# Twenty-nine instead of twelve filler transposes in the opening, one load for three constants, and a new order of the last scalings and stores

## The chip, the cores and the metric

The kernel runs on one core of a Trainium2 chip. The metric is the device time of one execution in microseconds (us), the median of the runs shown. Everything is computed in fp32; a matrix product is made of three products of a high and a low part (the type F32R in the code), so that one product of the reference is three matmuls on the chip.

## The reference, cut to what matters

The layer has 1024 latent tokens and 256 context tokens of width 1024. The parts that the change touches are the first and the last:

```python
c_silu = jax.nn.silu(c)[:, None, :]
cctx_silu = jax.nn.silu(c_ctx)[None, :]
sh1, sc1, g1, sh2, sc2, g2 = jnp.split(c_silu @ w_ada[l] + b_ada[l], 6, axis=-1)
hx = _modulate(_rmsnorm(x, norm1_g[l]), sh1, sc1)      # (y * g) * (1 + sc1) + sh1
(xq, xk, xv, ...) = jnp.split(hx @ w_in[l], IN_OFFSETS, axis=-1)
...                                                     # attention, retention, merge
x = x + g2 * _conv_ffn(hx2, w_up[l], conv_w[l], conv_b[l], w_down[l])
return _rmsnorm(x, final_norm_g)                        # y = x * rsqrt(mean(x*x) + EPS) * g
```

The inputs `c` and `c_ctx`, the bias `b_ada` and the gains `norm1_g`, `norm2_g` are the small constants of the change. The last RMSNorm, whose rows are scaled and stored at the very end, is its third part.

## The kernel before, in words

The work runs in stages: an opening (0 to about 60 us) that normalizes and transposes the tokens, computes the modulation and starts the first projection; then neighbourhood attention, retention, merge and the feed-forward network with its down projection (`steps`, and the last loop of the file), which ends with the final RMSNorm. TensorE (PE) is busy in nearly the whole span.

**The opening** is written out by hand as a list of small steps under `manual_schedule`, so that each engine gets its instructions in the order of the list. The steps that matter here:

- `load_x(tb)` brings a block of 128 tokens (512 KB) by the queue of SyncE (SP); `load_ag(g, q)` brings a piece of 512 KB of the modulation's weights, `load_f(half, t)` a piece of the first projection's weights, by the same queue. The framework gives every DMA of SP's and ACT's queues the next of eight semaphores in turn; a DMA that gets a semaphore for the second time is issued only when the DMA that had it before has landed. So the small loads of the constants take part in this rotation.
- `square_x` (ACT) sums the squares of a block, `rstd_x` (POOL) makes the factor, `scale_x` (DVE) scales the block, `transp(tb, kbs)` (line 213) transposes pieces of it on PE into PSUM.
- `silu_cc` (line 260) makes the SiLU of the two conditioning vectors; `ag_mm(g, q)` (line 291) multiplies them by a piece of modulation weights, 8 small matmuls side by side; `ag_ev` copies the rows out, `ag_tr` (line 301) turns them into columns, `ag_fin` (lines 307 and 308) adds the bias and multiplies by the gain.
- `split_hi`, `split_lo` split weights in two parts, `mod_h`, `mod_v`, `mod_l` make the modulated tokens in two parts, and `first_mm(half, kb)` (lines 130 to 132) is the first projection: 9 matmuls of 128x512 for one block of 128 channels.
- `turn_idle(to, n)` (line 203) puts n transposes of the identity matrix on PE. Nothing reads their result. They stand at two places before the change: 34 ahead of the first transpose of tokens, 12 ahead of `ag_mm(0, 0)`.

**The constants** come by ACT's queue, in three DMAs: `ccol` (64 bytes in each of 128 partitions, for `silu_cc`), `bcol` (192 bytes, the bias) and `gcol` (64 bytes, the gains). Behind them on ACT stands the first activation (line 257), which loads a table.

**The end.** The last 512 tokens are four row blocks, here b = 0 to 3, and of each the right half of the columns comes last. For b = 0 to 2 the loop makes the last matmuls of block b; `vec` (DVE) multiplies by the gate and subtracts (lines 2413, 2414); `square` (ACT, line 2323) sums the squares; `factor` (POOL, lines 2332, 2333) makes the reciprocal root; `scaled` scales the left half on ACT (line 2340) and the right half on DVE (line 2341) and stores both, 256 KB each. Block 3 goes in two halves of 256 columns (lines 2430, 2431, 2433). Before the change `scaled` of block 1 stands between the two halves of block 3, `scaled` of block 2 behind them, and `scaled` of block 3 alternates: scale left part, scale right part, store the left part by ACT's own queue, store the right part by SP's queue, twice.

Of the kernel before, what the change touches and what calls it, by code (L numbers as in the profile page):

```python
# [8 lines left out]
F32 = mybir.dt.float32  # L9
F32R = mybir.dt.float32r  # L10
AF = mybir.ActivationFunctionType
ALU = mybir.AluOpType
# [4 lines left out]
P = 128  # L17
D = 1024
KB = D // P
# [15 lines left out]
EPS = 1e-6  # L35
# [5 lines left out]
def tile_hybrid_layer(ctx, tc: tile.TileContext, io, dbg=None):  # L41
    nc = tc.nc
    vec, act, pool, pe, sync = nc.vector, nc.scalar, nc.gpsimd, nc.tensor, nc.sync

    def sb(name, side, bufs=1):
        return tc.alloc_tile_pool(name=name, bufs=bufs, side=side, reuse_waits="tile")
# [25 lines left out]
    cpool = sb("const", "left")  # L72
# [5 lines left out]
    def const(name, shape, queue=None):  # L78
        t = cpool.tile(shape, F32, name=name)
        (queue or sync).dma_start(t, io[name])  # L80
        return t
# [75 lines left out]
    s0 = sb("start", "right")  # L157
# [15 lines left out]
    def rstd_x(t0, n):  # L173
        r = rstd[:, t0 : t0 + n]
        pool.tensor_scalar(r, ssq[:, t0 : t0 + n], 1.0 / D, EPS, ALU.mult, ALU.add)
        pool.tensor_tensor(r, r, mhalf[:, t0 : t0 + n], ALU.pow)
# [16 lines left out]
    def p_tile(tag):  # L193
        return p0.tile([P, 512], F32, tag=tag, bufs=2 if tag == "tp" else 3, name=tag)
# [6 lines left out]
    def turn_idle(to, n):  # L201
        for _ in range(n):
            pe.transpose(to, ident, ident)

    def transp(tb, kbs, tags=None, idle=0):
        grid, half, i = tb < NTB, tb // 4 % 2 if tb < NTB else 0, tb % 4 if tb < NTB else tb - NTB
        for n, kb in enumerate(kbs):
            if i == 0 and (grid or kb % 2 == 0):
                tps[grid, half, kb] = p_tile(tags[n])
                if not grid:  # L210
                    tps[grid, half, kb + 1] = tps[grid, half, kb][:, C:]
            turn_idle(tps[grid, half, kb][:, i * P : (i + 1) * P], idle)
            pe.transpose(tps[grid, half, kb][:, i * P : (i + 1) * P], xs[tb][:, kb * P : (kb + 1) * P], ident)
# [30 lines left out]

    ccin = s0.tile([P, KB, 2], F32, name="ccin")
    ccol = s0.tile([P, KB, 32], F32, name="ccol")
    vec.memset(ccol, 0.0)
    cs2 = csp.tile([P, D], F32, name="cs")  # L250

    cst = {}
    act.dma_start(ccin, io["ccol"])
    for k, name, shape in (("b", "bcol", [P, 48]), ("g", "gcol", [P, 2, KB])):
        cst[k] = const(name, shape, act)

    act.activation(tick, mhalf[:, 0:1], AF.Silu)

# [16 lines left out]
    def load_ag(g, q):  # L275
        ag[g, q] = s_tile("x", 19)
        sync.dma_start(ag[g, q], io["w_ada1g"][sum(QS[:g]) + q])
# [6 lines left out]
    def ag_mm(g, q, idle=0):  # L284
        nk = len(GROUPS[g])
        if q == 0:
            arow[g] = p_tile("tp")
            turn_idle(arow[g][:, 0:P], idle)
        for n in range(4):
            k, r = (4 * q + n) // nk, slice(32 * n, 32 * n + 32)  # L290
            pe.matmul(arow[g][r, 0:256], ccol[:, k], ag[g, q][:, n * 256 : n * 256 + 256], start=q == 0, stop=q == QS[g] - 1, tile_position=(0, 32 * n))
# [33 lines left out]
    def split_hi(half, t):  # L325
        act.copy(first[t][half][:, 0], fraw[half, t])
# [328 lines left out]
    with tc.manual_schedule():  # L655
# [17 lines left out]
        transp(0, (5,), ("c1",))  # L673
        transp(0, (4,), ("c0",))
        transp(0, (1,), ("c0",))
        ag_mm(0, 0, idle=12)
        rstd_x(3, 1)
        load_ag(1, 0)
        square_x(1)
# [61 lines left out]
        ag_ev(2, "act")  # L741
        evac_t(True, 0, 4, "vec")
        load_ag(3, 0)
        transp(1, (2,), ("c1",))
        split_hi(0, 1)
        ag_tr(2)
        split_hi(0, 2)
        ag_mm(4, 0)
        load_ag(3, 1)
        split_lo(0, 1)  # L750
        ag_fin(2)
# [263 lines left out]
    bcol, gcol = cst["b"], cst["g"]  # L1015
# [346 lines left out]
    mix, last = None, (None, None)  # L1362
    share = shares()
    for h in range(RH):
        head = Head(h)
        for i in range(NCB + NTB):
# [3 lines left out]
            last = (head, i)  # L1370
# [247 lines left out]
    for n, (db, half) in enumerate(order):  # L1618
        if n in (5, 6):
            k = len(wpn) - KH  # L1620
# [68 lines left out]
    last = len(gu) - 1  # L1689
# [458 lines left out]
    with tc.manual_schedule():  # L2148
# [4 lines left out]
        ts, vr = slice(3 * P, 4 * P), [gtile(0, F32, "vr").rearrange("p (k t) -> p k t", t=P) for _ in range(2)]  # L2153
# [127 lines left out]
    fg = dp.tile([P, D], F32, name="fg")  # L2281
    sync.dma_start(fg, io["final_g"].to_broadcast([P, D]))
    gate2 = brow(3, dp.tile([P, D], F32, name="gate2"))
    ssf = dp.tile([P, NTB, 6], F32, name="ssf")
    QB = NTB // 2
# [21 lines left out]
    def gs(dh):  # L2307
        return slice(dh * 512, dh * 512 + 512)
# [11 lines left out]
    part = {}  # L2320

    def square(tb, dh, junk):
        act.activation(junk, part[tb, dh], AF.Square, accum_out=ssf[:, tb, dh : dh + 1])

    def early_part(tb, dh):
        s, z = ssf[:, tb], part[tb, dh]
        pool.tensor_scalar(s[:, 2:3], s[:, dh : dh + 1], 1.0 / D, EPS, ALU.mult, ALU.add)
        pool.tensor_tensor(z, z, fg[:, gs(dh)], ALU.mult)

    def factor(tb, c):  # L2330
        s = ssf[:, tb]
        pool.tensor_scalar(s[:, 3:4], s[:, c : c + 1], 1.0 / D, s[:, 2:3], ALU.mult, ALU.add)
        pool.tensor_tensor(s[:, 4:5], s[:, 3:4], mhalf[:, 0:1], ALU.pow)

    def scaled(tb, dh):
        s, ts = ssf[:, tb], slice(tb * P, (tb + 1) * P)
        z0, z1 = part[tb, 1 - dh], part[tb, dh]
        last = tb == QB - 1
        for c in (slice(0, 256), slice(256, 512)) if last else (slice(0, 512),):
            act.activation(z0[:, c], z0[:, c], AF.Copy, scale=s[:, 4:5])  # L2340
            vec.scalar_tensor_tensor(z1[:, c], z1[:, c], s[:, 4:5], fg[:, gs(dh)][:, c], ALU.mult, ALU.mult)
            (act if last else sync).dma_start(io["out"][ts, gs(1 - dh)][:, c], z0[:, c])
            sync.dma_start(io["out"][ts, gs(dh)][:, c], z1[:, c])

    def finish(tb, dh):
        factor(tb, dh)
# [14 lines left out]
    for b in range(QB):  # L2361
        x, z = rows_of(b, 0), dw_tile("x2", NTB)
# [14 lines left out]
    for b in range(QB):  # L2377
        x, z = rows_of(QB + b, 1), dw_tile("x2", NTB)
# [8 lines left out]
    for b in range(QB):  # L2387
        tb = QB + b
        x, z = rows_of(tb, 0), dw_tile("z", 6)
# [9 lines left out]
    with tc.manual_schedule():  # L2399
        tl = [operands(6, j) for j in range(NH - NL, NH)]  # L2400
        halves = (slice(0, 256), slice(256, 512))
        for b in range(QB):
            ts = slice(b * P, (b + 1) * P)
            z, junk = dw_tile("z", 6), dw_tile("xr", 4)
            part[b, 1] = z
            if b == QB - 1:
                break
            for i, (a, w) in enumerate(tl):
                open3(banks[0][b], a[:, 0, ts], a[:, 1, ts], w[:, 0], w[:, 1], False, i == NL - 1)
            if b == 0:  # L2410
                for tb in range(NTB - 3, NTB):
                    finish(tb, 0)
            vec.tensor_tensor(z, banks[0][b], gate2[:, gs(1)], ALU.mult)
            vec.tensor_tensor(z, p1[b], z, ALU.subtract)
            square(b, 1, junk)
            if b == 0:
                rest = p1[QB - 1]
                vec.tensor_tensor(u2[QB - 1], banks[0][QB - 1], gate2[:, gs(1)], ALU.mult)
                vec.tensor_tensor(rest, rest, u2[QB - 1], ALU.subtract)
            else:  # L2420
                factor(b - 1, 1)
                if b < QB - 2:
                    scaled(b - 1, 1)
        ends = [pd[1].tile([P, 512], F32, tag="y", bufs=4, name="y")[:, 0:256] for _ in halves]
        for bank, c in zip(ends, halves):
            for i, (a, w) in enumerate(tl):
                open3(bank, a[:, 0, ts], a[:, 1, ts], w[:, 0, c], w[:, 1, c], i == 0, i == NL - 1)
        factor(b - 1, 1)
        for n, (bank, c) in enumerate(zip(ends, halves)):
            vec.tensor_tensor(z[:, c], bank, gate2[:, 512 + c.start : 512 + c.stop], ALU.mult)  # L2430
            vec.tensor_tensor(z[:, c], rest[:, c], z[:, c], ALU.subtract)
            k = 5 if n else 1
            act.activation(junk[:, c], z[:, c], AF.Square, accum_out=ssf[:, b, k : k + 1])
            if not n:
                s = ssf[:, b]
                pool.tensor_scalar(s[:, 2:3], s[:, 1:2], 1.0 / D, s[:, 2:3], ALU.mult, ALU.add)
                scaled(b - 2, 1)
        scaled(b - 1, 1)
        factor(QB - 1, 5)
        scaled(QB - 1, 1)  # L2440
    pd[1].release()
    pd[0].release()
    dp.release()
# [9 lines left out]
def layout(inputs):  # L2453
    import numpy as np

    g = {k: np.asarray(v) for k, v in inputs.items()}
    ac = np.ascontiguousarray
    out = {"x": ac(g["x"][0]), "ctx": ac(g["ctx"][0])}
    cols = lambda v: v.reshape(-1, P).T
    out["cvec"] = ac(np.stack([g["c"][0], g["c_ctx"]]))  # L2460
    w_ada, b_ada = g["w_ada"][0], g["b_ada"][0]
    out["bcol"] = ac(cols(b_ada))
    out["gcol"] = ac(np.stack([cols(g["norm1_g"][0]), cols(g["norm2_g"][0])], 1))
    w1 = w_ada[:, :2048]
    single = w1.reshape(2, 4, P, 2, KB, P).transpose(4, 0, 2, 1, 3, 5)[:4].reshape(8, P, 1024)
    double = w1.reshape(4, 2, P, 2, NPE, 2 * P).transpose(4, 0, 2, 1, 3, 5)[2:].reshape(8, P, 1024)
    out["w_ada1g"] = ac(np.concatenate([single, double]))
    out["ccol"] = ac(out["cvec"].reshape(2, KB, P).transpose(2, 1, 0))
    out["w_ada2"] = ac(w_ada[:, 2048:].T.reshape(32, P, D))
    out["norm2"] = ac(g["norm2_g"])  # L2470
    out["final_g"] = ac(g["final_norm_g"][None])
# [81 lines left out]
```

## Time and profile before

| what | value |
|---|---|
| median of 3 runs | 1699.91 us (1699.9 to 1700.0) |
| the profiled execution | 1699.26 us |
| its span, from the first to the last instruction | 1697.5 us |
| mean granted TensorE clock | 0.998 |
| PE busy | 1681.8 us, 99% |
| DVE, ACT, POOL busy | 1256.9, 846.0, 570.6 us |

The profile's times are microseconds from the start of the span. PE is the matmuls, PEld the loads of their weights, DVE VectorE, ACT ScalarE, POOL GpSimd, SP SyncE; a name with q behind it (SPq, ACTq) is that engine's queue, which issues DMAs. Of the views, the page gives totals, the chain of waits goes back from the last instruction through what released each step, the timeline lists instructions with their start, duration and, in brackets, the idle time of the engine before them and what ended it; the windows give busy time, granted clock (PEclk) and DMA traffic of chosen stretches. Matmuls overlap: a row "x12" lasts from the start of the first to the end of the last.

### The profile page before, as it was taken

To read this page: it belongs to the slowest core of one execution; us is meant where nothing else is said; L and a number is where in the kernel's file an instruction comes from. 1 tells how busy PE (TensorE), PEld (TensorE's weight loads), DVE (VectorE), ACT (ScalarE), POOL (GpSimd) and SP (SyncE) were. 2 spreads that over 40 slices of the span, in tenths; PEclk is the share of its full clock that TensorE was granted. 3 is DMA by queue.
4 is the path that set the end of the run, shared out by engine and by line. 5 is a ranking of instruction groups with operands and counts; after the bars stand their busy time and mean duration, and the time that the engine had idled before them with its cause. 6 is when DMAs were issued, how large, how long until landed. Compare 5 with 4: busy or idle time off the path is not lost.

```text
span 1697.5 us, 25362 instructions
## 1 busy us (share of the span) xinstructions
PE 1681.8 (99%) x8328; PEld 1406.9 (83%) x8328; DVE 1256.9 (74%) x2485; ACT 846.0 (50%) x1778; POOL 570.6 (34%) x740
## 2 busy tenths in 40 slices
PE   9999999999999999999999999999999999999998
PEld 6888888888888888888888888888888888888886
DVE  5777786665788777566657876897888998847756
ACT  6665665553454444353446343754444444635444
POOL 2101233222344353013320221023666666411444
PEclk9999999999999999999999999999999999999999
DMA  9356788862465643799979976977666756998754
GB/s 383 101 154 164 187 201 221 217 176 62 141 164 138 193 84 98 255 328 333 312 223 309 268 207 203 303 228 219 174 194 180 202 168 195 263 305 297 242 158 177
DMA packets 174053, 357.66 MB, mean 211 GB/s; under 512 B 30945, under 2 KB 51457, under 8 KB 166561
## 3 DMA queue, kind: packets, MB, share of 16 engines
q1 hardware_dynamic: 136464, 263.34, 45.6%
q0 software_dynamic: 22272, 77.71, 23.3%
q10 hardware_dynamic: 15184, 14.99, 2.6%
q8 instruction: 66, 1.08, 0.3%
q14 instruction: 67, 0.54, 0.1%
HBM read 279.62 MB, written 150.26 MB: 253 GB/s over the span
## 4 chain that ended last, share of the span: by engine, by line
PE 84%; issue 5%; DMA 4%; POOL 3%; DVE 2%; ACT 1%; SPq 0%; POOLq 0%; ACTq 0%; DVEq 0%
PE u L1445 33%; PE mm L130 4%; PE mm L131 4%; PE mm L132 4%; PE mm L121 4%; PE mm L120 4%; PE mm L119 4%; PE pr L1445 4%; PE y L1445 2%; PE R L519 2%; PE ptp L501 2%; PE om L130 2%; PE om L131 2%; PE om L132 2%; DMA ur<-d_a 1%
## 5 line engine op out<-in xcount | busy, mean ns | idle before, releaser
L1445 PE MATMUL u<-T,wc 128*128 128x512 f32 x1056 | 246.3, 389 | 0.3 <-DVE T L96 0.2
L1445 PEld LDWEIGHTS u<-T,wc 128*128 128x128 f32 x1056 | 198.0, 188 | 42.3 <-DVE T L96 0.6
L1445 PE MATMUL y<-wc,ahl 128*128 128x512 f32 (+1 forms) x936 | 210.0, 386 | 0.4 <-DVE wc L96 0.4
L1445 PEld LDWEIGHTS y<-wc,ahl 128*128 128x128 f32 x936 | 174.1, 188 | 36.4 <-DVE wc L96 0.8
L96 DVE TENSOR_TENSOR wc<-ur,wc 128x512 fp32r<-128x512 f32 x171 | 126.5, 743 | 45.3 <-ACT wc L95 45.3
L95 ACT CAST wc<-ur 128x512 fp32r<-128x512 f32 x171 | 105.8, 623 | 108.3 <-PE u L1445 59.6
L120 PE MATMUL mm<-low,wc 128*128 128x512 f32 (+1 forms) x312 | 119.2, 382 | 0.0
L1445 PE MATMUL u<-h2a,wc 128*128 128x512 f32 x504 | 118.2, 389 | 0.0
L1445 PEld LDWEIGHTS u<-h2a,wc 128*128 128x128 f32 x504 | 94.5, 188 | 19.6
L531 POOL DMA_DIRECT2D d_ona<-rs x32 | 32.1, 1004 | 223.6 <-DVE st L492 49.6
L119 PE MATMUL mm<-hx,wc 128*128 128x512 f32 x264 | 107.2, 406 | 0.0
L121 PE MATMUL mm<-hx,wc 128*128 128x512 f32 x264 | 104.9, 397 | 0.0
L1445 PE MATMUL u<-hxT,wc 128*128 128x512 f32 x384 | 90.0, 389 | 0.0
L590 POOL COPY pad<-pu 128x1 f32<-128x1 f32 x62 | 39.6, 638 | 147.8 <-DVE pu L1486 110.8
L1445 PEld LDWEIGHTS u<-hxT,wc 128*128 128x128 f32 x384 | 72.1, 188 | 14.9
L95 ACT CAST wc<-wr 128x512 fp32r<-128x512 f32 x69 | 42.8, 622 | 67.0 <-PE u L1445 53.8
L96 DVE TENSOR_TENSOR ahl<-ur,ahl 128x512 fp32r<-128x512 f32 x66 | 52.4, 801 | 24.8 <-ACT ahl L95 24.7
L95 ACT CAST wc<-s 128x512 fp32r<-128x512 f32 x56 | 34.9, 623 | 68.5 <-PE u L1445 66.4
L132 PE MATMUL mm<-wc,low 128*128 128x512 f32 (+1 forms) x180 | 68.8, 382 | 0.0
L95 ACT CAST wc<-raw 128x512 fp32r<-128x512 f32 x77 | 47.9, 624 | 35.0 <-PE u L1445 5.6
L120 PEld LDWEIGHTS mm<-low,wc 128*128 128x128 f32 x312 | 59.1, 189 | 7.5
L1199 ACT ACTIVATE kz<-r,dec 128x128 fp32r<-128x128 f32 x72 | 27.4, 401 | 71.1 <-POOL r L1180 70.8
(440 smaller groups left out, 4648.1 us busy)
## 6 DMA issues: line engine op xcount, KB each, us to landing
d_a<-at SPq DMA_DIRECT2D x77, 256.0 KB, 6.1
ur<-d_a SPq DMA_DIRECT2D x77, 256.0 KB, 5.2
ur<-in_w_up SPq DMA_DIRECT2D x76, 256.0 KB, 6.2
d_w<-in_w_down POOLq DMA_DIRECT2D x66, 256.0 KB, 6.9
aw<-in_w_ada SPq DMA_DIRECT2D x32, 512.0 KB, 4.9
d_a<-d_a POOLq DMA_DIRECT2D x44, 256.0 KB, 7.3
ur<-d_w SPq DMA_DIRECT2D x44, 256.0 KB, 3.6
ur<-in_w_down SPq DMA_DIRECT2D x33, 256.0 KB, 6.1
```

Source lines behind the costliest of these rows:

```text
L95: act.copy(hi, src)
L96: (lo_eng or vec).tensor_tensor(lo, src, hi.bitcast(F32), ALU.subtract)
L119: pe.matmul(out, wh, xh, start=k == 0, stop=False)
L120: pe.matmul(out, wh, xl, start=False, stop=False)
L121: pe.matmul(out, wl, xh, start=False, stop=k == n - 1)
L130: pe.matmul(out, ah, bh, start=first, stop=False)
L131: pe.matmul(out, ah, bl, start=False, stop=False)
L132: pe.matmul(out, al, bh, start=False, stop=last)
L501: pe.transpose(tp[:, c], self.Pm[h][:, c * P : (c + 1) * P], ident)
L519: pe.matmul(R[:, h], self.pair.V[:, g, h].rearrange("p a b -> p (a b)"), self.PT[h][:, c].rearrange("p a b -> p (a b)"), start=c == 0, sto ...
L590: late(pool.tensor_copy(tick, src))
L1445: pe.matmul(out, a, b, start=first and n == 0, stop=last and n == 2, skip_group_check=True)
```

## The change

It has three parts. First, `turn_idle` gets 17 instead of 12 turns ahead of `ag_mm(0, 0)`, and two new places with 6 turns each: ahead of the transpose of block 1, piece 2, which stands before `ag_tr(2)`, and ahead of `ag_mm(4, 0)`. Second, the three constants are laid side by side by the host (320 bytes in each partition) and come in one DMA. Third, at the end, the left half of block 1 is scaled and stored by ACT and SP before the squares of block 2; its right half as before between the halves of block 3; block 3's four quarters are scaled back to back, two on ACT and two on DVE, and stored only then, three by SP's queue and the last by ACT's. The division by 1024 in the mean moves from POOL into the scale factor of ACT's squares.

```diff
-    ccin = s0.tile([P, KB, 2], F32, name="ccin")
+    cols = cpool.tile([P, 2 * KB + 64], F32, name="cols")
+    ccin = cols[:, 0 : 2 * KB].rearrange("p (k s) -> p k s", s=2)
...
-    cst = {}
-    act.dma_start(ccin, io["ccol"])
-    for k, name, shape in (("b", "bcol", [P, 48]), ("g", "gcol", [P, 2, KB])):
-        cst[k] = const(name, shape, act)
+    act.dma_start(cols, io["cols"])
+    cst = {"b": cols[:, 2 * KB : 2 * KB + 48], "g": cols[:, 2 * KB + 48 :].rearrange("p (n k) -> p n k", n=2)}
...
-        ag_mm(0, 0, idle=12)
+        ag_mm(0, 0, idle=17)
...
-        transp(1, (2,), ("c1",))
+        transp(1, (2,), ("c1",), idle=6)
         split_hi(0, 1)
         ag_tr(2)
         split_hi(0, 2)
-        ag_mm(4, 0)
+        ag_mm(4, 0, idle=6)
...
     def square(tb, dh, junk):
-        act.activation(junk, part[tb, dh], AF.Square, accum_out=ssf[:, tb, dh : dh + 1])
+        act.activation(junk, part[tb, dh], AF.Square, scale=D ** -0.5, accum_out=ssf[:, tb, dh : dh + 1])
...
-        pool.tensor_scalar(s[:, 2:3], s[:, dh : dh + 1], 1.0 / D, EPS, ALU.mult, ALU.add)
+        pool.tensor_scalar(s[:, 2:3], s[:, dh : dh + 1], EPS, None, ALU.add)
...
-        pool.tensor_scalar(s[:, 3:4], s[:, c : c + 1], 1.0 / D, s[:, 2:3], ALU.mult, ALU.add)
+        pool.tensor_scalar(s[:, 3:4], s[:, c : c + 1], s[:, 2:3], None, ALU.add)
...
+    def scaled_a(tb, dh, c=slice(0, 512), queue=None):
+        z = part[tb, 1 - dh]
+        act.activation(z[:, c], z[:, c], AF.Copy, scale=ssf[:, tb, 4:5])
+        store(tb, 1 - dh, c, queue)
+
+    def scaled_b(tb, dh, c=slice(0, 512)):
+        z = part[tb, dh]
+        vec.scalar_tensor_tensor(z[:, c], z[:, c], ssf[:, tb, 4:5], fg[:, gs(dh)][:, c], ALU.mult, ALU.mult)
+        store(tb, dh, c)
+
+    def store(tb, dh, c, queue=None):
+        (queue or sync).dma_start(io["out"][tb * P : (tb + 1) * P, gs(dh)][:, c], part[tb, dh][:, c])
...
+            if b == QB - 2:
+                factor(b - 1, 1)
+                scaled_a(b - 1, 1)
             square(b, 1, junk)
...
-            if not n:
-                s = ssf[:, b]
-                pool.tensor_scalar(s[:, 2:3], s[:, 1:2], 1.0 / D, s[:, 2:3], ALU.mult, ALU.add)
-                scaled(b - 2, 1)
-        scaled(b - 1, 1)
-        factor(QB - 1, 5)
-        scaled(QB - 1, 1)
+            if n:
+                scaled_a(b - 1, 1)
+                scaled_b(b - 1, 1)
+            else:
+                pool.tensor_tensor(sb[:, 2:3], sb[:, 1:2], sb[:, 2:3], ALU.add)
+                scaled_b(b - 2, 1)
+        factor(b, 5)
+        for z, dh in ((part[b, 0], 0), (part[b, 1], 1)):
+            for c in halves:
+                if dh:
+                    vec.scalar_tensor_tensor(z[:, c], z[:, c], sb[:, 4:5], fg[:, gs(1)][:, c], ALU.mult, ALU.mult)
+                else:
+                    act.activation(z[:, c], z[:, c], AF.Copy, scale=sb[:, 4:5])
+        store(b, 1, halves[0])
+        store(b, 0, halves[0])
+        store(b, 1, halves[1])
+        store(b, 0, halves[1], act)
```

More of the change, by code (lines that the diff above doesn't have):

```diff
@@ L2331, in factor @@
         s = ssf[:, tb]
-        pool.tensor_scalar(s[:, 3:4], s[:, c : c + 1], 1.0 / D, s[:, 2:3], ALU.mult, ALU.add)
+        pool.tensor_scalar(s[:, 3:4], s[:, c : c + 1], s[:, 2:3], None, ALU.add)
         pool.tensor_tensor(s[:, 4:5], s[:, 3:4], mhalf[:, 0:1], ALU.pow)
-    def scaled(tb, dh):
[L2336 to L2343, printed above, removed]
+    def scaled_a(tb, dh, c=slice(0, 512), queue=None):
[8 more added lines that the diff above has]
+        (queue or sync).dma_start(io["out"][tb * P : (tb + 1) * P, gs(dh)][:, c], part[tb, dh][:, c])
+    def scaled(tb, dh):
+        scaled_a(tb, dh)
+        scaled_b(tb, dh)
     def finish(tb, dh):
@@ L2419, in tile_hybrid_layer @@
                 vec.tensor_tensor(rest, rest, u2[QB - 1], ALU.subtract)
-            else:
+            elif b < QB - 2:
                 factor(b - 1, 1)
-                if b < QB - 2:
-                    scaled(b - 1, 1)
+                scaled(b - 1, 1)
         ends = [pd[1].tile([P, 512], F32, tag="y", bufs=4, name="y")[:, 0:256] for _ in halves]
@@ L2428, in tile_hybrid_layer @@
         factor(b - 1, 1)
+        sb = ssf[:, b]
         for n, (bank, c) in enumerate(zip(ends, halves)):
@@ L2432, in tile_hybrid_layer @@
             k = 5 if n else 1
-            act.activation(junk[:, c], z[:, c], AF.Square, accum_out=ssf[:, b, k : k + 1])
-            if not n:
-                s = ssf[:, b]
-                pool.tensor_scalar(s[:, 2:3], s[:, 1:2], 1.0 / D, s[:, 2:3], ALU.mult, ALU.add)
-                scaled(b - 2, 1)
-        scaled(b - 1, 1)
-        factor(QB - 1, 5)
-        scaled(QB - 1, 1)
+            act.activation(junk[:, c], z[:, c], AF.Square, scale=D ** -0.5, accum_out=sb[:, k : k + 1])
+            if n:
[15 more added lines that the diff above has]
+        store(b, 0, halves[1], act)
     pd[1].release()
@@ L2461, in layout @@
     w_ada, b_ada = g["w_ada"][0], g["b_ada"][0]
-    out["bcol"] = ac(cols(b_ada))
-    out["gcol"] = ac(np.stack([cols(g["norm1_g"][0]), cols(g["norm2_g"][0])], 1))
     w1 = w_ada[:, :2048]
@@ L2467, in layout @@
     out["w_ada1g"] = ac(np.concatenate([single, double]))
-    out["ccol"] = ac(out["cvec"].reshape(2, KB, P).transpose(2, 1, 0))
+    ccol = out["cvec"].reshape(2, KB, P).transpose(2, 1, 0).reshape(P, 2 * KB)
+    out["cols"] = ac(np.concatenate([ccol, cols(b_ada), cols(g["norm1_g"][0]), cols(g["norm2_g"][0])], 1))
     out["w_ada2"] = ac(w_ada[:, 2048:].T.reshape(32, P, D))
```

## The prediction

> **What bounds the kernel now.** I read the page first: which engine is busy, and which holds the end.
>
> ```profile
> PE 1681.8 (99%) x8328; PEld 1406.9 (83%) x8328; DVE 1256.9 (74%) x2485; ACT 846.0 (50%) x1778; POOL 570.6 (34%) x740
> ...
> PE 84%; issue 5%; DMA 4%; POOL 3%; DVE 2%; ACT 1%; SPq 0%; POOLq 0%; ACTq 0%; DVEq 0%
> ```
>
> PE holds 84% of the chain. The change touches none of PE's work behind the opening, so it can win only where PE waits or runs slowly in the first 60 us, and behind the last matmul. The second view is the chain of waits of the opening (start, duration, what).
>
> ```profile
> 2.59 7.12 DMA x<-in_w_ada1g
> 9.72 10.42 DMA x<-in_w_ada1g
> 20.28 0.64 PE tp L291 x8
> ...
> 22.61 0.43 PE c L132
> ...
> 25.91 0.23 PE c L132
> ```
>
> Two things stand here. Up to 20.28 the chain is DMA: one piece of modulation weights, then, issued when that has landed, another. Behind it PE holds the chain, but the same 128x512 matmul takes 0.43 us at 22.61 and 0.23 us at 25.91. The third view, the windows, says why (PE, PEld, DVE, ACT and POOL busy, PEclk, DMA share, GB/s).
>
> ```profile
> 21.50:22.00 0.50, 0.50 (x4) 0.36 (x3) 0.50 (x1) 0.50 (x1) 0.00 (x0) 0.74 1.03 410
> 22.00:22.50 0.50, 0.50 (x3) 0.40 (x2) 0.50 (x2) 0.50 (x2) 0.00 (x0) 0.50 1.04 410
> 25.00:25.50 0.50, 0.50 (x3) 0.44 (x2) 0.00 (x0) 0.50 (x1) 0.50 (x1) 0.84 1.04 418
> 8.11:11.52 3.41, 2.37 (x28) 1.35 (x26) 1.82 (x4) 1.45 (x4) 1.70 (x4) 1.00 1.03 418
> 18.35:21.76 3.41, 2.09 (x16) 1.49 (x17) 1.83 (x6) 2.11 (x5) 0.00 (x0) 1.00 1.04 411
> ```
>
> PEclk is 0.50 from about 21.74 (0.74 over half a microsecond is 0.26 us of half clock) to 25.16 (0.84: 0.16 us): a dip of 3.4 us. The 3.41 us just before it had PE busy for 2.09 us; an earlier stretch of that length, with 2.37 us busy, was followed by no dip. So the line between lies, by this row, between 61% and 69% busy. The timeline of PE shows the pauses in those stretches, and the turns.
>
> ```profile
> 1.36 5.53 PE L203 MATMUL c<-ident 128*128 128x128 f32 x34 [1.36 <-POOL ident masks.py:199]
> 7.88 1.47 PE L203 MATMUL tp<-ident 128*128 128x128 f32 x12
> 9.84 0.64 PE L291 MATMUL tp<-x,ccol 128*32 128x256 f32 x8 [0.49 <-DMA x<-in_w_ada1g]
> 11.03 0.64 PE L291 MATMUL tp<-x,ccol 128*32 128x256 f32 x8 [0.55 <-DMA x<-in_w_ada1g]
> 18.97 0.61 PE L301 MATMUL tp<-sel,arow 128*128 128x2 f32 x4 [0.73 <-ACT arow L295]
> 20.28 0.64 PE L291 MATMUL tp<-x,ccol 128*32 128x256 f32 x8 [0.70 <-DMA x<-in_w_ada1g]
> ```
>
> The added turns stand exactly in the first, third and fourth of these pauses: 0.49, 0.73 and 0.70 us.
>
> **The turns.** Twelve turns last 1.47 us, the tail of the last one included, so one takes at most 1.47/12 = 0.12 us. Five more are 0.6 us, six are 0.73 us. In the first pause they end 0.1 us behind the landing that now ends it, and the next product waits for its own DMA anyhow (0.55 us idle before 11.03). In the other two they fit, 0.73 into 0.73 and 0.70. So they delay nothing by more than 0.1 us, as long as the clock is at full speed. The twelve of the later pauses add 1.4 us to the 2.09 us busy of the stretch before the dip, which fills the 3.41 us, far over 69%. If turns count as work for the clock, the dip goes.
>
> Do they? The 34 opening turns are the only work of PE up to 6.89 us, and the clock came up under them. The windows of the turns alone (PE, PEld, PEclk, share, GB/s) show how many lie in half a microsecond:
>
> ```profile
> 4.00:4.50 0.50, 0.50 (x4) 0.50 (x3) 1.00 1.06 409
> 5.50:6.00 0.50, 0.50 (x7) 0.50 (x6) 1.00 1.00 382
> ```
>
> Four before 4.5 us, seven after 5.5: the rate nearly doubles, with nothing on PE but turns (PEclk says 1.00 for both, the record of the clock seems to begin with the first change). So the trace says that turns count. [...] I follow the rows.
>
> What the dip costs: 3.4 us at half clock do the work of 1.7 us, so 1.7 us is the upper bound. Less remains where PE, running ahead, meets something that doesn't come sooner. The nearest such things:
>
> ```profile
> 28.88 0.75 DVE L179 TENSOR_SCALAR x<-x,rstd 128x1024 f32<-128x1024 f32 x1 [0.72 <-POOL rstd L176]
> 28.92 0.64 PE L291 MATMUL tp<-x,ccol 128*32 128x256 f32 x8
> 30.64 0.98 PE L213 MATMUL c<-ident,x 128*128 128x128 f32 x7
> 16.80 4.36 SPq L277 DMA_DIRECT2D x<-in_w_ada1g  x4
> DMA to landing us min/median/max: 3.4/7.8/10.4
> ```
>
> The last token block of the first eight is scaled until 28.88 + 0.75 = 29.63; its first transpose is the third of the seven at 30.64, two transposes of 0.12 us later at 30.88. It can come forward by 1.2 us, no more, since the scaling hangs on a DMA, a square and POOL, not on PE. The weights for the product at 28.92 were issued at 16.80 and have landed by 27.2 even with the longest flight of 10.4 us, which leaves 1.7 us. Behind that, ACT and DVE work on what PE delivers and come forward with it. I take 1.2 us, the bound of the scaling, with 0.7 and 1.7 as ends. What comes next is PE-bound, so a start that is earlier by 1.2 us should reach the end undiminished.
>
> **The packed constants.** Their loads cost no engine time that matters: ACT issues three DMAs instead of one, but its first square waits for a token block anyhow. What they cost is DMA time, and the opening's chain is DMA.
>
> ```profile
> 4.14 1.06 ACT L171 ACTIVATE v<-x 128x1024 f32<-128x1024 f32 x1 [0.50 <-DMA x<-in_x]
> 5.62 1.06 ACT L171 ACTIVATE v<-x 128x1024 f32<-128x1024 f32 x1 [0.33 <-DMA x<-in_x]
> 7.25 1.06 ACT L171 ACTIVATE v<-x 128x1024 f32<-128x1024 f32 x1 [0.38 <-DMA x<-in_x]
> q10 hardware_dynamic: 432, 0.04, 3.6%
> ```
>
> The first three token blocks of 512 KB land at about 4.1, 5.6 and 7.2; two more such pieces land by 9.71 and the next by 11.03, 1.26 us each on the mean. So the second and third block took 3.11 us where 2.52 would do: 0.6 us lost while the small packets of `bcol` and `gcol` ran beside them. That is the upper bound. The lower: in the first 9 us (the DMA view of that stretch, the row with q10) ACT's queue held 3.6% of the DMA engines' time, 0.32 us, and two of its three loads go: 0.2 us. I take 0.4 us, in the middle. SP's loads, which take turns with ACT's on the eight semaphores, stand behind a token block's landing where they stood behind `bcol`'s and `gcol`'s; I count nothing for that, since the DMA engines have pieces queued in either case. All landings of the opening, the one at 20.14 on the chain among them, move forward by that 0.4 us, and the chain with them; there the six turns end 0.1 us after the landing at worst. That one landing now serves all three readers costs nothing: the first of them, the SiLU on ACT, stands behind the squares of two token blocks (5.62 + 1.06), and its load is still the first on its queue.
>
> **The end.** The rows behind the last matmul, then the DMA traffic from 1680 in slices of 0.44 us.
>
> ```profile
> 1688.42 0.63 ACT L2323 ACTIVATE xr<-z 128x512 f32<-128x512 f32 x1 [1.38 <-DVE z L2414]
> 1690.71 0.42 ACT L2433 ACTIVATE xr<-z 128x256 f32<-128x256 f32 x1 [0.27 <-DVE z L2431]
> 1691.74 0.55 POOL L2333 TENSOR_TENSOR ssf<-ssf,mhalf 128x1 f32<-128x1 f32 x1
> 1691.86 0.33 SPq L2342 DMA_DIRECT2D out_dram<-x  x1
> 1692.29 1.40 SPq L2343 DMA_DIRECT2D out_dram<-z  x3
> 1693.80 0.34 ACTq L2342 DMA_DIRECT2D out_dram<-x  x1
> DMA  3999999950000010009992000199999999970000
> out_dram<-x ACTq DMA_DIRECT2D x2, 128.0 KB, 2.5
> ```
>
> The square at 1690.71 waits for DVE, not for ACT, so taking block 1's scaling off ACT there brings it no sooner; its new place costs nothing either, since ACT idles 1.38 us before 1688.42 and a pass over 512 columns takes 0.63 us (that row). POOL's factor ends at 1692.29 as before; its two small operations keep their number, and one of them loses a multiplication on a single column, which I count at nothing. From there ACT's second part no longer stands behind its own DMA issue (0.34 us), but the third of SP's last stores now stands in a line: 1692.29 and four issues of 1.40/3 = 0.47 us, the last beginning near 1693.7, against ACT's last at 1693.80. That is 0.1 us. The DMA row says why it is not more: the engines are full from slice 26, 1691.4, to 1695.6, and of these 4.2 us only block 1's 512 KB go ahead into idle slices; blocks 2 and 3, 1 MB, can't begin before the issue at 1691.86 and its flight. A 128 KB store flies 2.5 us in the crowd, so the last lands at about 1696.2 instead of 1696.3. I take 0.1 us, between 0 and 0.5. The factor 1/1024 inside ACT's square is a scale that the instruction has anyhow: nothing.
>
> **The sum.** 0.4 + 1.2 + 0.1 = 1.7 us off the span of 1697.5, whose execution took 1699.26 in all; the 1.76 us around the span stay. The median of the runs is 0.65 us above that execution; I take the difference off the median: 1699.91 - 1.7 = 1698.2 us.
>
> **The rivals.**
>
> First, the dip stays: turns don't count, or the timed executions had no dip to lose, or it moves to another place. For it speaks only that one execution is profiled; against it the doubled rate under the opening turns. Then 0.5 us is left: 1699.4 us. Chance 0.22. [...]
>
> Second, more than I take: PE meets no bound and wins all 1.7 us, the constants give 0.6 and the end 0.5: 2.8 us, 1697.1 us. For it speaks that the chain of waits stays on PE behind 20.28; against it the scaling at 28.88. Chance 0.15.
>
> Third, slower: the turns themselves hold PE at half clock. If the stretch up to 17.6 us is already judged idle, each of the twelve late turns takes twice 0.12 us, 2.9 us in pauses of 0.73 + 0.70, so the chain from there on comes 1.5 us late, the landings' 0.4 us is hidden behind the turns, and only the end's 0.1 us is won: 1701.3 us. It decides where PE's busy share falls below some 65% before 17.6; the nearest that the rows show is the 69% that held. Chance 0.06.
>
> **How the numbers follow.** The forecast has 0.57, with its own range from 1697.5 to 1699.0 by the ends of the three terms. To hold 8 in 10 the range goes to the first rival and close to the second: 1696.9 to 1700.0. A measurement of this kernel tells some 0.2% from no change, 3.4 us, more than any of these terms; so nearly all cases are "same": 0.93. Faster than 1696.5 needs more than the second rival, 0.05; slower than 1703.3 needs more than the third, 0.02.
>
> **What would show it.** PEclk 1.00 in all windows from 18 to 30, and the first-projection matmuls 0.23 us apart from the first on; a wait of PE for DVE's scaling near 28; ACT's squares of the third block near 6.8 instead of 7.25 and the product of 20.28 near 19.9; the last store's issue near 1693.7 relative to an unmoved end of PE. I am wrong if PEclk still falls, if PE at 60 us is less than 0.8 us ahead, or if the DMA slices at the end show an idle gap before the last stores.

## The result and the profile after

| | before | after |
|---|---|---|
| median (6 runs each) | 1699.91 us | 1710.51 us |
| lowest and highest | 1698.23, 1700.13 | 1709.55, 1711.47 |
| profiled execution, its span | 1699.26, 1697.5 | 1710.21, 1708.4 |

The changed kernel is slower: ratio 1.0065, 95% interval 1.0052 to 1.0078, or 10.6 us. The forecast was 1.7 us in the other direction, and no rival came near. The page of the kernel after (totals, shares of the chain, two groups of matmuls: count, busy us, mean ns of one, idle):

```profile
PE 1694.1 (99%) x8345; PEld 1405.4 (82%) x8345; DVE 1260.5 (74%) x2485; ACT 843.3 (49%) x1778; POOL 573.7 (34%) x740
...
PE 82%; DMA 5%; issue 5%; POOL 3%; DVE 3%; ACT 1%; POOLq 0%; SPq 0%; ACTq 0%; DVEq 0%
...
L1444 PE MATMUL u<-T,wc 128*128 128x512 f32 x1056 | 252.9, 394 | 0.0
...
L1444 PE MATMUL u<-h2a,wc 128*128 128x512 f32 x504 | 118.7, 390 | 0.0
```

The same two groups on the page of the kernel before:

```profile
L1445 PE MATMUL u<-T,wc 128*128 128x512 f32 x1056 | 246.3, 389 | 0.3 <-DVE T L96 0.2
...
L1445 PE MATMUL u<-h2a,wc 128*128 128x512 f32 x504 | 118.2, 389 | 0.0
```

PE is busy for 12.3 us more, so nearly all of the time was lost in PE's own work and not in waits. Two groups of the same shape, one source line and one set of weights (`wc`) behave differently: with `T` as the other operand, 1056 matmuls take 6.6 us more; with `h2a`, next to nothing changes. The timeline of PE in one stretch of the feed-forward network shows it (start, duration, operands, count). Before:

```profile
1204.61 5.60 PE L1445 MATMUL u<-h2a,wc 128*128 128x512 f32 x24
1210.05 8.32 PE L1445 MATMUL u<-T,wc 128*128 128x512 f32 x36
1218.21 0.39 PE L1445 MATMUL u<-h2h,wc 128*128 128x512 f32 x1
```

After:

```profile
1209.32 5.62 PE L1444 MATMUL u<-h2a,wc 128*128 128x512 f32 x24
1214.78 8.56 PE L1444 MATMUL u<-T,wc 128*128 128x512 f32 x36
1223.17 0.39 PE L1444 MATMUL u<-h2h,wc 128*128 128x512 f32 x1
```

From the start of the 36 to the next start are 8.16 us before (0.2267 us each) and 8.39 us after (0.2331). The 24 with `h2a` keep 5.44 and 5.46 us. PEclk is 1.00 in both (windows 1204.60 to 1218.30 before, 1209.30 to 1223.30 after). Following the same matmul through both traces shows where the time goes:

| before's time of the matmul, us | after comes earlier (-) or later (+), us | main matmuls of the stretch that ends there |
|---|---|---|
| 59 | -1.51 | opening |
| 721 | -1.35 | attention, retention |
| 898 | +1.86 | `u<-hxT,wc` x384, with `hx`, `low` |
| 1013 | +1.96 | `pr<-xop,wc` |
| 1482 | +10.79 | `u<-T,wc` x1056, `h2h` x176, `h2l` x88, with `h2a` |
| 1689 | +10.88 | `y<-wc,ahl` |

From 1013 to 1482 after loses 8.83 us; 1320 matmuls (1056 + 176 + 88) at 6.5 ns, the difference of the intervals as the single starts give it (0.2333 - 0.2268), are 8.6. From 721 to 898 it loses 3.21 us; 384 at 6.5 ns are 2.5. Together 1704 matmuls, 11.1 us. One more group behaves alike, 192 matmuls `pn<-ona,wc` between 692 and 736 us, two thirds of them ahead of the row at 721. One of its three lines, before and then after:

```profile
L119 PE MATMUL pn<-ona,wc 128*128 128x512 f32 x64 | 25.1, 392 | 0.0
```

```profile
L119 PE MATMUL pn<-ona,wc 128*128 128x512 f32 x64 | 25.5, 398 | 0.0
```

With them 1896 matmuls are slower, which at 6.5 ns each is some 12 us, nearly all of the 12.4 that after loses from 59 to 1689.

**The opening came as forecast.** The windows from 18 to 30 us (PE, PEld, DVE, ACT, POOL busy, PEclk, DMA share, GB/s), before and then after:

```profile
18.00:30.00 12.00, 10.57 (x55) 7.56 (x52) 8.13 (x14) 7.90 (x14) 4.10 (x8) 0.86 1.03 408
```

```profile
18.00:30.00 12.00, 11.83 (x82) 8.46 (x80) 8.60 (x16) 7.61 (x14) 4.10 (x8) 1.00 1.03 409
```

PEclk goes from 0.86 to 1.00: the dip is gone. The chain of waits of after says what binds then:

```profile
28.51 0.76 DVE x L179
29.32 0.77 PE c L213 x5
```

It is DVE's scaling of the last token block, as forecast. The last of these token transposes, which began at 65.6 us before, begins at 64.2 in the list of after's instructions by source line (duration min/median/max, first to last start):

```profile
L213 PE MATMUL tp<-ident,x x28: 270/272/329, 7.6 to 64.2; 128*128 128x128 f32 x28
```

**The end** moved with PE. The timeline of after's last stores:

```profile
1703.17 0.94 SPq L2345 DMA_DIRECT2D out_dram<-z  x2
...
1704.19 0.37 ACTq L2345 DMA_DIRECT2D out_dram<-x  x1
1704.70 0.41 SPq L2345 DMA_DIRECT2D out_dram<-z  x1
```

The last store is issued at 1704.70; before it was 1693.80, and with PE's 10.88 us later that is 1704.68. From the start of the last matmul to the end of the span are 8.05 us, before 8.03. The new order brought nothing that shows.

### The profile page after: what moved, and what is told of

It is laid out like the page before. It is cut to its first block, busy times and chain, and to the rows that moved or that the text cites. A ratio compares the mean times of both kernels' runs of the same rounds, so it can differ in the third digit from the quotient of the medians.

```text
span 1708.4 us, 25392 instructions
## 1 busy us (share of the span) xinstructions
PE 1694.1 (99%) x8345; PEld 1405.4 (82%) x8345; DVE 1260.5 (74%) x2485; ACT 843.3 (49%) x1778; POOL 573.7 (34%) x740
## 4 chain that ended last, share of the span: by engine, by line
PE 82%; DMA 5%; issue 5%; POOL 3%; DVE 3%; ACT 1%; POOLq 0%; SPq 0%; ACTq 0%; DVEq 0%
PE u L1444 34%; PE mm L130 4%; PE mm L132 4%; PE mm L131 4%; PE pr L1444 4%; PE mm L121 3%; PE mm L120 3%; PE mm L119 3%; PE y L1444 2%; PE R L518 2%; PE ptp L500 2%; PE om L132 2%; PE om L130 2%; PE om L131 2%; DMA ur<-d_a 2%
## 5 line engine op out<-in xcount | busy, mean ns | idle before, releaser
L1444 PE MATMUL u<-T,wc 128*128 128x512 f32 x1056 | 252.9, 394 | 0.0
L96 DVE TENSOR_TENSOR wc<-raw,wc 128x512 fp32r<-128x512 f32 x77 | 54.7, 717 | 11.4 <-ACT wc L95 10.8
```

What stands on the lines that cost most here:

```text
L96: (lo_eng or vec).tensor_tensor(lo, src, hi.bitcast(F32), ALU.subtract)
L1444: pe.matmul(out, a, b, start=first and n == 0, stop=last and n == 2, skip_group_check=True)
```

## The experiments

What separates `T` from `h2a`? In the program's allocation the persistent pools, which hold PE's operands, grow from two sides of each partition of SBUF. `wc`, `hx`, `h2a`, `ahl` and `xop` stand on the left, `T`, `hxT`, `ona`, `h2h` and `h2l` on the right. The new tile `cols` has 80 columns in the left pool; `bcol` and `gcol` had 64 there, and `ccin`, with 16, lay in a pool of the opening. So everything on the left behind it starts 64 bytes later (`wc` at 3008 instead of 2944, `h2a` at 33728 instead of 33664), and the right stays (`T` at 104320). Theory: a matmul is slower when its two operands start at a wrong distance. Rival: something else in the change slows PE. Each run is shown beside runs of the kernel before on the same chip (medians 1699.3, 1698.87 and 1698.48 us for E1 to E4, E5 to E8 and E9 to E12).

**E1. Before, with only the left side moved by 64 bytes.**

```diff
-    tick = cpool.tile([P, 16], F32, name="pad")[:, 0:1]
+    tick = cpool.tile([P, 32], F32, name="pad")[:, 0:1]
```

> The kernel before, with nothing but its first padding tile widened from 16 to 32 fp32 columns, so that every tile that is laid out from the left side of SBUF starts 64 bytes further, as the wider tile of constants makes it do in the changed kernel. Theory (placement): the two operands of a matmul lie 64 bytes apart modulo 128 where one is on the left and one on the right; those matmuls follow each other in 0.2334 instead of 0.2270 us, about 1700 of them: +11 us, 1710 to 1712 us, and PE in the window 1200:1480 has about 1210 matmuls instead of 1237. Rival (timing): the changed kernel is slow because PE runs 1.5 us ahead and its reads then meet other traffic; nothing of that is here, so 1699.9 us and 1237 matmuls.

Measured: 1710.38 us, ratio 1.0067 (1.0052 to 1.0082). Timeline of PE:

```profile
1208.82 5.62 PE L1445 MATMUL u<-h2a,wc 128*128 128x512 f32 x24
1214.28 8.56 PE L1445 MATMUL u<-T,wc 128*128 128x512 f32 x36
```

An unused piece of 64 bytes makes the whole loss, in the same matmuls.

**E2. After, with the 64 bytes taken back.**

```diff
-    tick = cpool.tile([P, 16], F32, name="pad")[:, 0:1]
-    ex = cpool.tile([P, 5], F32, name="ex")
+    ext = cpool.tile([P, 8], F32, name="ex")
+    ex, tick = ext[:, 0:5], ext[:, 7:8]
```

> The changed kernel with the 64 bytes taken back: the junk column of the first activation moves into the spare columns of another tile, and its 16 columns go, so that all tiles behind the constants start where they started before. Theory (placement): the loss goes and the opening's gain of 1.5 us stays: 1697.5 to 1698.8 us, 1237 matmuls in a full window of 280 us. Rival (timing): still about 1710 us.

Measured: 1699.87 us, ratio 1.0003 (0.9994 to 1.0012).

```profile
1204.78 5.60 PE L1444 MATMUL u<-h2a,wc 128*128 128x512 f32 x24
1210.22 8.32 PE L1444 MATMUL u<-T,wc 128*128 128x512 f32 x36
```

The loss is gone, with everything else of the change in place. The gain that was expected to stay is not there: nothing is left to measure, though PE is 1.57 us ahead at 59 us.

**E3 and E4. Is the unit 128 bytes?** E3 moves after's left side by 64 bytes more, E4 moves its right side by 64 bytes the other way; both make a distance of 128 bytes.

```diff
-    tick = cpool.tile([P, 16], F32, name="pad")[:, 0:1]
+    tick = cpool.tile([P, 32], F32, name="pad")[:, 0:1]
```

> The changed kernel with 16 more columns of padding, so that the left tiles start 128 bytes behind their old place. Theory (placement modulo 128): as fast as with the 64 bytes taken back, 1697.5 to 1698.8 us. If any move of the left tiles costs, or if 256 bytes are the unit: about 1710 us. Rival (timing): about 1710 us.

```diff
-    edge.tile([P, 24], F32, name="pad")
+    edge.tile([P, 40], F32, name="pad")
```

> The changed kernel with 16 more columns of padding on the right side of SBUF as well, so that left and right tiles are both moved by 64 bytes modulo 128. Theory (the distance of the two operands counts): 1697.5 to 1699 us. Rival (each tile by itself must start at a multiple of 128 bytes): slower than the changed kernel, since the right tiles are off too: 1715 us or more. Rival (timing): about 1710 us.

Measured: E3 1711.38 us, 1.0074 (1.0058 to 1.0091); E4 1711.21 us, 1.0074 (1.0059 to 1.0089). Both expectations of a fast kernel missed. One row of each timeline, E3 first:

```profile
1215.68 8.55 PE L1444 MATMUL u<-T,wc 128*128 128x512 f32 x36
```

```profile
1215.69 8.55 PE L1444 MATMUL u<-T,wc 128*128 128x512 f32 x36
```

At 128 bytes the loss is as large as at 64. If there is a unit, it is larger.

**E5, E6, E7. 256 bytes, both sides together, 32 bytes.** E5 is after with its left side 256 bytes behind before's, E6 after with the right side moved by the same 64 bytes as the left, E7 before with its left side moved by only 32.

```diff
-    tick = cpool.tile([P, 16], F32, name="pad")[:, 0:1]
+    tick = cpool.tile([P, 64], F32, name="pad")[:, 0:1]
```

> The changed kernel with 48 more columns of padding, so that the left tiles start 256 bytes behind their old place. Theory (the distance of the two operands modulo 256 counts): fast, 1698 to 1700 us, u matmuls on right tiles 0.227 us apart. Rivals (any move of the left tiles, or a unit of 512 bytes or more): about 1711 us.

```diff
-    edge.tile([P, 24], F32, name="pad")
+    edge.tile([P, 8], F32, name="pad")
```

> The changed kernel with 16 columns less of padding on the right side, so that the right tiles move by 64 bytes the way in which the left ones moved: the two sides are at the same distance as before, but no tile starts at a multiple of 128 bytes. Theory (distance modulo 256): fast, 1698 to 1700 us. Rival (each tile's own start counts): 1711 us or more.

```diff
-    tick = cpool.tile([P, 16], F32, name="pad")[:, 0:1]
+    tick = cpool.tile([P, 24], F32, name="pad")[:, 0:1]
```

> The kernel before with the left tiles moved by 32 bytes only. Theory (distance modulo 256, whatever its size): slow, 1709 to 1712 us. Rival (the unit of a read is 64 bytes, smaller moves stay in it): 1699 us; anything between would say that the loss grows with the distance.

Measured, one run each: E5 1700.63, E6 1699.73, E7 1712.99 us. Timelines in this order:

```profile
1211.33 8.32 PE L1444 MATMUL u<-T,wc 128*128 128x512 f32 x36
```

```profile
1210.40 8.32 PE L1444 MATMUL u<-T,wc 128*128 128x512 f32 x36
```

```profile
1217.56 8.56 PE L1445 MATMUL u<-T,wc 128*128 128x512 f32 x36
```

A shift of 256 bytes leaves the 36 matmuls at 8.32 us, so by these runs the distance counts modulo 256. Moving both sides leaves them there too, so it is the distance, not where each starts. And 32 bytes cost these matmuls as much as 64 or 128 (8.56, 8.56 and 8.55 us): it is a step, not a slope.

**E8. Before, with only the seventeen added turns.**

```diff
-        ag_mm(0, 0, idle=12)
+        ag_mm(0, 0, idle=17)
...
-        transp(1, (2,), ("c1",))
+        transp(1, (2,), ("c1",), idle=6)
...
-        ag_mm(4, 0)
+        ag_mm(4, 0, idle=6)
```

> The kernel before with the 17 added turns alone, every tile at its old place. If the turns keep the clock up in every execution: all runs at a granted clock of 0.999 and near the 1698.4 us of the undipped runs of before (whose dipped runs take 1699.5), ratio 0.9994 to the mixture. Rival (the dip is a matter of the windows' phase and the turns don't prevent it): runs of 0.998 and 0.999 mixed, about 1699.5 us, ratio 1.000.

Measured: 1699.41 us, ratio 1.0002 (0.9992 to 1.0011). The window that would have brought a dip (its place, and the phase of which the rival speaks, are explained with E12):

```profile
16.83:20.24 3.41, 2.36 (x29) 1.49 (x21) 2.48 (x5) 1.67 (x3) 0.00 (x0) 1.00 1.03 405
```

No dip, and no gain that can be told from nothing: PE is 0.67 us ahead of before's profile at 59 us and 0.49 us behind it at 1689. The expectation took an execution's mean clock as a sign of the dip; that doesn't hold: this profile has 0.998 without one, since the half clock behind the last matmul counts in the mean too (before's profile has PEclk 0.50 there, from 1694.4 to 1697.5 us).

**E9. A probe**: eight blocks of 96 matmuls on one core, the first to warm up; beside each of the others run only ACT's copy of the last block's result (0.59 us) and its store. Moving operand and weights come from two tiles on the left that start 4096 bytes apart, a multiple of 256; beyond that the distance is `da` 0 bytes, `db` 32, `dc` 64, `dd` 128, `de` 256. `own` alternates so that the matmul's own weights are always 64 bytes off, `nxt` so that the next one's are.

```
run(y, [(0, 0)])             # da: moving offset, weight offset in floats
run(y, [(0, 8)])             # db
run(y, [(0, 16)])            # dc
run(y, [(0, 32)])            # dd
run(y, [(0, 64)])            # de
run(y, [(0, 16), (16, 0)])   # own
run(y, [(0, 0), (16, 16)])   # nxt
```

> A probe that computes nothing of the layer: blocks of 96 matmuls of 128x512 (the type of the kernel's operands), back to back with no other engine at work, weights and moving operand in two tiles of the same residue modulo 256; the blocks differ in the distance of the two operands: 0 (warm, da), 32 (db), 64 (dc), 128 (dd), 256 bytes (de). Theory (distance modulo 256): da and de 96 x 0.227 = 21.8 us a block, db, dc, dd 22.3 to 22.4 us. Rival (the loss needs the writes of the other engines): all blocks 21.8 us. Two more blocks tell which weights count: in own each matmul is 64 bytes from its own weights and 0 from those of the next one, in nxt the other way round. If the loading of the next weights, which runs beside the matmul, meets its reads: nxt slow (22.4 us) and own fast; if a matmul's own weights count, the reverse.

Measured: 192.04 us in all. Its chain of waits (start, duration):

```profile
30.79 21.77 PE da L30 x96
52.56 22.39 PE db L30 x96
74.95 22.40 PE dc L30 x96
97.35 22.32 PE dd L30 x96
119.67 21.77 PE de L30 x96
141.44 22.41 PE own L30 x96
163.84 22.25 PE nxt L30 x96
```

21.77/96 is 0.2268 us, 22.40/96 is 0.2333: the two intervals of the kernel, with the other engines nearly idle and both operands on one side. So the loss needs neither other engines' traffic nor two sides. One of `own` and `nxt` was expected to be fast; both are slow, so whose weights have to fit, this matmul's or the next one's, stays open.

**E10 and E11. The packed constants alone (with the layout kept as in E2), and the new end alone.** E10 is E2's edit and the change's lines for `cols` on the kernel before; E11 is the change's edits from `square` on.

> The kernel before with the constants packed into one load and nothing else, the 16 columns taken back elsewhere, so that every tile lies where it lay. Theory: the landings of the second and third token block come 0.2 to 0.6 us sooner and so does the chain up to the clock's dip or its absence; ratio 0.9998, not to be told from 1. Rival (the packing moves something else in the schedule): slower by 0.5 us or more.

> The kernel before with the new order of the last scalings and stores alone. The profile of the changed kernel had 8.05 us from the start of the last matmul to the end of the span, that of before 8.03. Theory (the last stores are bound by the DMA engines and the flight of the last one): 8.0 us again, ratio 1.000. Rival (the prediction's 0.1 to 0.5 us is there but hidden): 7.5 to 7.9 us.

Measured: E10 1698.15 us, 0.9998 (0.9989 to 1.0007); E11 1698.72 us, 1.0002 (0.9993 to 1.0011). E10's profile has the same dip as before's (at 21.39 us), so their opening can be compared: PE is 0.20 us ahead at 59 us. But so is E11's, 0.20 us, whose opening is that of before. From E11's last matmul to its end are 7.99 us instead of 8.03; in E10, with the old end, 7.66.

**E12. Before once more, with an empty line added**, for how much one profile of the same program differs from another.

> The kernel before once more, with an empty line added, for a second profile of its opening. If the dip belongs to the program: PEclk 0.50 for 3.4 us near 21.7 again. If it depends on where the clock's 3.4 us windows happen to fall (first grant at 4.68 with a dip, at 4.38 without one in the kernel before with moved tiles): as likely no dip as one, and the opening at 60 us is 1.1 to 1.3 us ahead of the first profile without any change.

Measured: 1698.43 us, one run, and no dip. Rows of the windows, first of E12, then of E11 (columns as above):

```profile
9.61:13.03 3.42, 2.20 (x24) 1.10 (x24) 1.58 (x3) 0.95 (x3) 1.16 (x3) 1.00 1.02 414
```

```profile
9.02:12.43 3.41, 1.78 (x22) 0.68 (x21) 1.59 (x3) 1.22 (x4) 1.67 (x4) 1.00 1.02 418
```

E11's dip lies at 12.43, directly behind the stretch shown, where the first profile of before has none. In the opening the thirteen profiles of the layer (before, after, E1 to E8, E10 to E12) fit one rule. By the trace's record of the clock the full clock is first granted at a time between 4.26 and 6.59 us that differs from execution to execution; call it the phase. Counted from there in steps of 3.413 us, the length that the same record gives for before's dip (PEclk 0.50 from 21.74 to 25.15 us), how busy PE is in one step goes with the clock of the next:

| profile | turns added | first grant, us | emptiest stretch up to 59 us: PE busy, us | dip from |
|---|---|---|---|---|
| before | no | 4.68 | 18.33 to 21.74: 2.07 | 21.74 |
| E10 | no | 4.32 | 17.97 to 21.39: 2.05 | 21.39 |
| E7 | no | 6.57 | 16.81 to 20.22: 1.98 | 20.22 |
| E11 | no | 5.61 | 9.02 to 12.43: 1.78 | 12.43 |
| E12 | no | 6.20 | 9.61 to 13.03: 2.20 | none |
| E1 | no | 4.38 | 7.79 to 11.21: 2.42 | none |
| E8 | yes | 6.59 | 16.83 to 20.24: 2.36 | none |
| E3, E6 | yes | 6.54, 5.55 | 2.44 each | none |
| after, E2, E4, E5 | yes | 4.26 to 4.83 | over 2.6 | none |

E7 and E8 are a pair to look at: the same phase within 0.02 us and the same stretch, with 1.98 us busy and a dip without the turns, 2.36 and none with them. The pair alone would not do, since busy time differs as much without turns: E1's phase, 4.38, lies between those of E10 and before, 4.32 and 4.68, but its stretch from 18.04 has 2.50 us busy where theirs have 2.05 and 2.07. What decides is how much of E8's 2.36 us are turns:

```profile
18.91 0.55 PE L213 MATMUL c<-ident,x 128*128 128x128 f32 x3
19.29 0.82 PE L203 MATMUL c<-ident 128*128 128x128 f32 x6
19.95 0.27 PE L213 MATMUL c<-ident,x 128*128 128x128 f32 x1
```

From 19.46, where the row before them ends, to 19.95 there is nothing else: 0.49 us. Without the turns 1.87 us are left, less than the 2.07 that brought a dip. In the kernel before, the stretch from 8.09 to 11.50 had 2.37 us busy, 1.26 of them in its twelve turns, and no dip behind it.

At the end of the program the same busy time did not bring the half clock. E11's last matmuls fill as much of a step as PE had before its dip, and the next step has the full clock; the half clock comes only behind that one, in which PE does nothing:

```profile
1688.36:1691.78 3.42, 1.78 (x15) 1.58 (x14) 3.29 (x7) 2.16 (x8) 1.53 (x3) 1.00 0.78 294
1691.78:1695.20 3.42, 0.00 (x0) 0.00 (x0) 0.99 (x3) 1.37 (x3) 0.86 (x2) 1.00 0.65 230
1695.20:1697.80 2.60, 0.00 (x0) 0.00 (x0) 0.00 (x0) 0.00 (x0) 0.00 (x0) 0.50 0.34 110
```

E3 (1.78 us) and E6 (1.88) end alike. So the line between 2.07 and 2.20 us holds for the mixed small work of the opening, not for any work; what exactly is counted stays open.

## Why the prediction was wrong

**The step that failed** stands in the first paragraph behind the page: "The change touches none of PE's work behind the opening, so it can win only where PE waits or runs slowly". It touches the place of one operand of 1896 matmuls there, which cost some 12 us. The working of the packed constants priced their load (DMA time, issues, who reads them) and nothing else; that their tile is 64 bytes larger than the two it replaces in its pool, ahead of the weights and much else that PE reads, was not looked at, so it stands in the sum at nothing without a reason. The kernel's lines 74 and 76 have a tile named `pad` at the head of either pool; the question what they pad was there to be asked. E1 and E2 show the cause from both sides, E3 to E7 and E9 its form. The range has a slip too: the ends of the three terms add up to 0.9 and 2.8 us, which is 1697.1 to 1699.0 us, not 1697.5.

**The turns** did what the working said: the clock counts them, the dip goes, and DVE's scaling binds next. PE was 1.51 us ahead at 59 us, of a forecast 1.6 (1.2 and 0.4). That it came so close is in part luck: the six profiles with the whole change are 0.98 to 1.57 us ahead, and E8, with the turns alone, 0.67. That the clock counts the turns is shown by their share of E8's stretch (0.49 of 2.36 us) and by no dip in seven profiles with turns against four in six without, as by the windows of before (four turns in half a microsecond, later seven).

**What the first rival had right** is that an execution may have no dip to lose. Two of six profiles without turns had none. A profile without a dip, E12 or E1, is 1.38 or 1.29 us ahead of before's at 59 us; E8 is only 0.54 us ahead of E7, its neighbour in phase with a dip. So the turns save 0.5 to 1.2 us in four of six executions, 0.8 us on the mean at most. The four dips begin 5, 5, 4 and 2 whole steps of 3.413 us behind the first grant, which itself lay at 4.68, 4.32, 6.57 and 5.61 us. In the opening PE busy for 2.07 of 3.41 us was not enough to keep the full clock, while at the end of E11 1.78 us were.

**"Should reach the end undiminished"** did not hold. E2 is 1.57 us ahead at 59 us and 0.28 behind at the end; E12, with no edit that matters, keeps 0.93 of its 1.38. A place where some is lost is at 141 us, in the waits of PE between 60 and 160 us of E5 (total, times, longest):

```profile
PE ptp L500 <- ACT P L489: 0.9, 1, 0.9
```

After has 0.4 us there and E2 0.2, before, E1 and E12 none. That PE now arrives too early can't be all: E1 and E12 are nearly as far ahead and lose at most 0.02 us. The chain of E5 says what ACT's softmax waits for, a piece of modulation weights that DVE works on first:

```profile
132.47 6.22 DMA aw<-in_w_ada
...
138.71 1.24 DVE aw L542 x2
139.94 0.09 DVE st L487
...
140.14 0.72 ACT P L489 x2
...
140.90 0.55 PE ptp L500 x3
```

In all seven profiles with the turns this load takes 5.4 to 6.2 us from its issue to its landing, and PE loses 0.2 to 1.1 us between 59 and 141; in the six without it takes 3.8 to 4.5, and PE loses at most 0.04. E8 differs from before by the turns alone and is one of the seven. So the turns go with a cost further on; what ties them to that load is not shown. E2 lost 0.3 more near 500 us, as did E12, and 0.5 near 1067. That is seen, not tested.

**The small terms**: the packed load moves the third token block's square to 7.03 to 7.14 us in the seven profiles that have it, against 7.18 to 7.90 in the six others (forecast: 6.8 instead of 7.25). What of it reaches 59 us is not shown, since E10's 0.20 us are no more than E11's. The end is worth nothing that can be told (0.02 us more in after, 0.04 less in E11, while E10's old end alone differs by 0.37) instead of 0.1, as small as forecast. In all, without the 64 bytes the change is E2: no difference that the runs can tell. No experiment gave a version that beats the kernel before by a measurable amount.

## What to carry to other kernels

A tile's size is part of a change: one that grows or moves shifts all tiles laid out behind it, so compare the start addresses of what the bounding engine reads before pricing anything else. When busy time of the bounding engine grows and no wait is new, split its instructions by operand, not by line, until one group keeps its time and its neighbour doesn't. And what one profile shows of the clock's dips is one phase of several: count them over several profiles before pricing their removal.

## What the runs showed of the hardware

- A 128x512 matmul that loads its weights anew each time follows the last every 0.2268 us when moving operand and weights start at the same address modulo 256 bytes (E9's `da` and `de`; in the layer before, E2, E5 and E6), and every 0.2325 to 0.2333 us, up to 2.9% later, at the other distances tried, 32, 64 and 128 bytes. In the probe nothing but the distance of the two changed, and the pace did; by what way the distance acts is not shown.
- In the opening the clock is halved for one step of 3.41 us behind a step in which PE was busy for 1.78 (E11), 1.98 (E7), 2.05 (E10) or 2.07 us (before, 61%), and not behind 2.20 us (E12, 64%) or more. At the end of the program it is not halved behind 1.78 us of dense 128x512 matmuls (E11, E3) or 1.88 (E6); behind 0.88 us (E8) it is.
- Transposes of the identity count as work for the clock: 2.36 us busy of which 0.49 are turns (E8), or 2.37 of which 1.26 are (before), kept the full clock.
